# Norm chains between the stages: elementwise work moved from GpSimd to VectorE

## The chip, the cores and the metric

The kernel runs on one core of one Trainium2 chip, as one launch. The metric is the device time of that launch in microseconds (us). A core has a matrix engine (TensorE, PE in the profile; its weight loads are PEld), an engine for elementwise work on two inputs (VectorE, DVE), one for functions of one input with a scale and a bias (ScalarE, ACT), a programmable one that can do elementwise work too (GpSimd, POOL), and queues that start transfers (SyncE, SP, and POOL's own). Each engine runs its instructions strictly in the order in which they were written; engines wait for each other through semaphores. The order here is written by hand: no scheduler moves anything.

## What is computed

Two layers of a diffusion backbone over 640 tokens of width 1024: 128 context tokens and 512 latent tokens, which differ in their conditioning vector. Cut to what matters:

```
def layer(x, cond, l, P, ctx, rope):
    mods = (silu(cond) @ w_mod[l] + b_mod[l])            # 9 vectors: shift, 1+scale, gate, three times
    def pre(x_, s):
        return rmsnorm(x_, g_pre[l, s]) * (1 + mods[3*s+1]) + mods[3*s]
    f = swiglu(pre(x, 0), ...);  x = x + 0.5 * mods[2] * rmsnorm(f, g_post[l, 0])
    m = token_mix(pre(x, 1));    x = x +       mods[5] * rmsnorm(m, g_post[l, 1])
    f = swiglu(pre(x, 2), ...);  x = x + 0.5 * mods[8] * rmsnorm(f, g_post[l, 2])
```

So there are six stages (F, M, F, F, M, F: a feed-forward or the token mixer), and between two of them the same two norms: the sum of squares of the stage's output f gives r1, then x = x + gain * r1 * f; the sum of squares of the new x gives r2, and h = gain * r2 * x + shift is the next stage's input. All is fp32. A matrix product is made of three: each fp32 operand is split into a high part (rounded to the format that TensorE takes) and a low part (the rest), and high*high, high*low and low*high are added up.

## The kernel before

The activations lie transposed, features on the 128 partitions: a token array is 8 chunks (c = 0 to 7) of 128 x 640. The 640 tokens are worked in two halves of 320 columns. Half 0 holds the 128 context tokens and 192 latent ones, so an instruction with a gain for each kind of token falls into a 128-column and a 192-column one; half 1 is one piece of 320 columns.

Weights come by SP's queue into `raw`; `split` (line 240) makes the high part `wh` on ACT (a cast) and the low part `wl` on DVE (a subtraction, line 243). `run` goes through a list of tasks: each task first splits the weights that are wanted one or two tasks later, then writes deferred work (`flush`), then some steps of a generator that runs beside the matmuls (`step`), and at last its own matmuls. That order is the order on each engine.

At a boundary between two stages (`boundary`, line 533) the last products of the old stage (its tail) are made for a first half of the tokens, then for the second; the first half's norms run as the generator `chain` (line 401) beside the tail of the second half, and the second half's beside the head of the next stage. `STEPS` says how many steps of a chain stand before each task. A chain goes:

- `rms_r`: a product of ones with the squares (line 339) sums them over the partitions, then r1 on ACT and DVE (lines 321 to 329, `s` is r).
- Eight steps for x: POOL makes t = f * r1 (line 414, two chunks ahead), DVE x = t * gain + x (line 450; two instructions in half 0), and two chunks later ACT squares the new x (line 423) and the square is added to a sum (line 425): for the first half on DVE into one sum, for the second by turns on POOL and DVE into two sums.
- The product with ones again, now for r2.
- Eight steps for h. Odd chunks: DVE makes h = x * gain * r2 (line 488), ACT adds the shift and rounds to the high part (line 490), DVE makes the low part (line 505, one step later). Even chunks: POOL makes x * r2 (line 414), ACT (and DVE for the context tokens, line 496) applies gain and shift (line 498), ACT rounds (line 499), DVE subtracts (line 509).

`evac_branch` (line 516) takes a stage's output from PSUM: ACT copies it to f and squares it (line 528), POOL adds the squares up (line 529), for 7 of 8 chunks in each half. `sums` (line 627), at the beginning of each feed-forward, recombines the two parts of the input for a scheme that saves products: for each of 4 chunk pairs two adds of 128 x 640 on POOL (line 637), then four of 128 x 320 on DVE (lines 638 to 641) and a split. `x` and `f` are the slots A to D by turns, and the next input's high and low part (`hn`) are the two others.

After the last stage the boundary has only the x steps; there DVE does chunks 0 and 3 of the second half alone (`solo`: line 447 f * gain * r1, line 452 x + t), and POOL the other products.

Of the kernel before, what the change touches and what calls it, by code (L numbers as in the profile page):

```python
# [80 lines left out]
class Kernel:  # L81
# [319 lines left out]
    def chain(self, hf, ahead, kind, post=None, pre=None, out=None):  # L401


        nc = self.nc
        s = slice(hf * HW, (hf + 1) * HW)
        acc = self.acc[:, s]
        loc = lambda b, e: slice(b - hf * HW, e - hf * HW)
        nxt = None

        def scaled(src, c, r):  # L410
            if c >= KC:
                return None
            t = self.t3()
            nc.gpsimd.tensor_mul(t, src[:, c, s], r)
            return t


        accs = (acc,) if ahead else (self.ssq[:, s], acc)
        n = len(accs)

        def square(c, q):
            a = accs[c % n]
            nc.scalar.activation(a if c < n else q, self.x[:, c, s], AF.Square)
            if c >= n:
                (nc.vector if ahead or c % 2 else nc.gpsimd).tensor_add(a, a, q)

        if post is not None:
            l, st = post
            ge = self.co[l][:, 3 + st]
            r1 = self.R[:, s]  # L430
            self.rms_r(r1, (self.ssq[:, s],), 0.25 / D)

            solo = lambda c: pre is None and not ahead and c in (0, 3)
            q1 = lambda c: None if c < KC and solo(c) else scaled(self.f, c, r1)
            nxt = [q1(0), q1(1)]
            yield
        qs = []
        for c in range(KC):
            if post is not None:
                q = nxt.pop(0)  # L440
                nxt.append(q1(c + 2))
                if solo(c):
                    q = self.t3()
                for (b, e, cd) in self.segs(hf):
                    x, t, gain = self.x[:, c, b:e], q[:, loc(b, e)], ge[:, c, cd:cd + 1]
                    if solo(c):
                        nc.vector.scalar_tensor_tensor(t, self.f[:, c, b:e], gain, r1[:, loc(b, e)],
                                                       op0=ALU.mult, op1=ALU.mult)
                    else:
                        nc.vector.scalar_tensor_tensor(x, t, gain, x, op0=ALU.mult, op1=ALU.add)  # L450
                if solo(c):
                    nc.vector.tensor_add(self.x[:, c, s], self.x[:, c, s], q)
            if out is not None:
                nc.sync.dma_start(out[:, c, s], self.x[:, c, s])
            if pre is not None:
                qs.append((c, q))
                if len(qs) > LAG:
                    square(*qs.pop(0))
            yield
        if pre is None:  # L460
            return
        for q in qs:
            square(*q)
        yield
        l, st = pre
        r2 = self.R[:, s]
        self.rms_r(r2, accs, 1.0 / D)
        late = nxt = None

        alone = lambda c: c % 2 == 1  # L470

        def first(c):
            return scaled(self.x, c, r2) if c < KC and not alone(c) else None

        nxt = [first(0), first(1)]
        yield
        if self.hn is None:
            self.hn = (self.slot(self.hs[0], F32R), self.slot(self.hs[1], F32R))
        for c in range(KC + 1):
            new = None  # L480
            if c < KC:
                h = nxt.pop(0)
                nxt.append(first(c + 2))
                if alone(c):
                    h = self.t3()
                    for (b, e, cd) in self.segs(hf):
                        hs = h[:, loc(b, e)]
                        nc.vector.scalar_tensor_tensor(hs, self.x[:, c, b:e], self.co[l][:, st, c, cd:cd + 1],  # L488
                                                       r2[:, loc(b, e)], op0=ALU.mult, op1=ALU.mult)
                        nc.scalar.activation(self.hn[0][:, c, b:e], hs, AF.Identity, bias=self.shift(l, st, c, cd))  # L490
                else:
                    for (b, e, cd) in self.segs(hf):
                        hs = h[:, loc(b, e)]
                        gain, shift = self.co[l][:, st, c, cd:cd + 1], self.shift(l, st, c, cd)
                        if cd == 0:
                            nc.vector.tensor_scalar(hs, hs, gain, shift, op0=ALU.mult, op1=ALU.add)
                        else:
                            nc.scalar.activation(hs, hs, AF.Identity, bias=shift, scale=gain)
                    nc.scalar.copy(self.hn[0][:, c, s], h)
                new = (c, h)  # L500
            if late is not None:
                k, hk = late
                if alone(k):
                    for (b, e, cd) in self.segs(hf):
                        nc.vector.scalar_tensor_tensor(self.hn[1][:, k, b:e], hk[:, loc(b, e)], self.shift(l, st, k, cd),
                                                       self.hn[0][:, k, b:e].bitcast(F32),
                                                       op0=ALU.add, op1=ALU.subtract)
                else:
                    nc.vector.tensor_sub(self.hn[1][:, k, s], hk, self.hn[0][:, k, s].bitcast(F32))  # L509
            late = new  # L510
            yield
# [4 lines left out]
    def evac_branch(self, ps, c, hf):  # L516

        nc = self.nc
        s = slice(hf * HW, (hf + 1) * HW)
        nc.scalar.copy(self.f[:, c, s], ps[:, hf, :HW])  # L520
        f, ssq = self.f, self.ssq

        def squares():
            if c == 0:
                nc.scalar.activation(ssq[:, s], f[:, c, s], AF.Square)
            else:
                q = self.t3()
                nc.scalar.activation(q, f[:, c, s], AF.Square)
                nc.gpsimd.tensor_add(ssq[:, s], ssq[:, s], q)

        self.later.append(squares)

# [58 lines left out]
    def ffn(self, l, st, mod_todo, first=False):  # L591

        a, nc = self.a, self.nc
# [13 lines left out]
        def spill():  # L607

            nc.gpsimd.dma_start(self.d_x, self.x)
            self.gens["sums"] = sums()  # L610
# [16 lines left out]
        def sums():  # L627

            sa, sb = (self.slots.tile([P, 4, KC // 2, HW], F32R, tag=t, name=self.nm("s")) for t in (self.xs, self.fs))
            S["S"] = [(sa[:, i], sb[:, i]) for i in range(4)]  # L630
            one, two = slice(0, HW), slice(HW, T)
            f = lambda t: t.bitcast(F32)
            dve = nc.vector
            for k in range(KC // 2):
                a1, a2, s31, s24 = (self.t6() for _ in range(4))
                for d, c in ((a1, k), (a2, KC // 2 + k)):
                    nc.gpsimd.tensor_add(d, f(self.h[0][:, c, :]), f(self.h[1][:, c, :]))
                dve.tensor_sub(s31[:, two], a1[:, two], a2[:, two])
                dve.tensor_sub(s31[:, one], a1[:, one], a1[:, two])
                dve.tensor_sub(s24[:, one], s31[:, two], a1[:, one])  # L640
                dve.tensor_add(s24[:, two], a2[:, one], s24[:, one])
                yield
                v = lambda t: t.rearrange("p (a b) -> p a b", a=2)
                for i, t in ((2, s24), (0, s31)):
                    self.split(sa[:, i:i + 2, k, :], sb[:, i:i + 2, k, :], v(t))
                yield
# [120 lines left out]
        if first:  # L767
            def first_fn(*ws):
                p = [self.ps() for _ in ws]
                self.projs(list(zip(p, ws)), KC, self.h, (0, 1), hook=self.first_hook)  # L770
                self.advance(False, 5)
                self.st.close()
                begin()
                self.gens["sums"] = sums()
                new_act(0)
                gate_out(0, p[0], (0, 1))
                up_out(0, p[1], (0, 1))
                gate_out(1, p[2], (0, 1))
            mid.append(Task("first", first_fn, (wg[0, 0], wg[0, 1], wg[1, 0]), ahead=0))
            mid.append(up(1, 1, (0, 1)))  # L780
# [936 lines left out]
```

## Time and profile before

| | us |
|---|---|
| three runs: median (lowest to highest) | 3232.16 (3231.4 to 3234.57) |
| the profiled execution, its own time | 3228.82 |
| its span, first to last instruction | 3227.0 |
| TensorE busy | 3042.9 (94%) |
| VectorE busy | 2334.3 (72%) |
| ScalarE busy | 1436.4 (45%) |
| GpSimd busy | 1079.7 (33%) |
| mean granted TensorE clock | 0.981 of full |

How to read it: TensorE is busy nearly all the time, so what it waits is what can be won or lost, beside the 16 us after its last product; the waits lie in the boundaries, at the beginning and in a few other places. "PE ps L339 <- POOL s L425" means that TensorE's instruction of line 339 waited for GpSimd's of line 425. A row of a time line has the start, the duration and the engine, then line, operation, tiles (buffer numbers left out) and shapes; xN are N such instructions in a row, whose time is the sum. TensorE's clock has two levels, 2.4 GHz (1.00) and 1.2 GHz (0.50).

### The profile page before, as it was taken

To read this page: it belongs to the slowest core of one execution; us is meant where nothing else is said; L and a number is where in the kernel's file an instruction comes from. 1 tells how busy PE (TensorE), PEld (TensorE's weight loads), DVE (VectorE), ACT (ScalarE), POOL (GpSimd) and SP (SyncE) were. 2 spreads that over 40 slices of the span, in tenths; PEclk is the share of its full clock that TensorE was granted. 3 is DMA by queue.
4 is the path that set the end of the run, shared out by engine and by line. 5 is a ranking of instruction groups with operands and counts; after the bars stand their busy time and mean duration, and the time that the engine had idled before them with its cause. 6 is when DMAs were issued, how large, how long until landed. Compare 5 with 4: busy or idle time off the path is not lost. (4 is left out here: it accounts for less than half of the span.)

```text
span 3227.0 us, 51500 instructions
## 1 busy us (share of the span) xinstructions
PE 3042.9 (94%) x20278; PEld 2986.2 (93%) x20278; DVE 2334.3 (72%) x3282; ACT 1436.4 (45%) x2535; POOL 1079.7 (33%) x841
## 2 busy tenths in 40 slices
PE   7999998999999989999989999989999999899997
PEld 6999998899999979999979999979999998899997
DVE  7878768876666597787686788678666666866665
ACT  4344356454432354343554343564444324544344
POOL 4245344500011244354444354344000113343344
PEclk9999999999999999999999999999999999999999
DMA  4436653311234444536544436542111444345344
GB/s 178 166 110 186 165 169 119 133 58 60 68 112 148 154 150 158 158 118 175 181 152 157 151 119 179 180 152 93 60 55 61 144 140 163 139 133 140 104 130 153
DMA packets 140213, 433.45 MB, mean 134 GB/s; under 512 B 16834, under 2 KB 34050, under 8 KB 139076
## 3 DMA queue, kind: packets, MB, share of 16 engines
q1 hardware_dynamic: 119380, 351.34, 32.6%
q0 software_dynamic: 20304, 78.66, 9.1%
q8 instruction: 159, 2.61, 0.3%
q14 instruction: 82, 0.67, 0.1%
q10 hardware_dynamic: 288, 0.17, 0.0%
HBM read 377.51 MB, written 52.59 MB: 133 GB/s over the span
## 5 line engine op out<-in xcount | busy, mean ns | idle before, releaser
L243 DVE TENSOR_TENSOR wl<-raw,wh 128x1024 fp32r<-128x1024 f32 (+3 forms) x525 | 645.0, 1231 | 432.5 <-ACT wh L242 425.2
L311 PE MATMUL ps<-act,wh 128*128 128x320 f32 x2816 | 570.1, 313 | 29.5 <-DVE act L243 10.8
L242 ACT CAST wh<-raw 128x1024 fp32r<-128x1024 f32 (+3 forms) x525 | 481.2, 919 | 78.9 <-PE ps L311 39.1
L311 PEld LDWEIGHTS ps<-act,wh 128*128 128x128 f32 x2816 | 457.7, 190 | 38.2 <-DVE act L243 14.1
L665 PE MATMUL ps<-s,wh 128*128 128x320 f32 x1920 | 445.4, 311 | 26.7 <-DVE t L689 26.7
L375 DVE CUSTOM_DVE_ANT_0 t<-wm,sc,par 128x1024 bf16<-128x1024 f32 x256 | 373.2, 1493 | 10.0 <-DMA wm<-in_w_mod 9.9
L311 PE MATMUL ps<-slotA,wh 128*128 128x320 f32 x1312 | 366.4, 317 | 14.3 <-ACT wh L242 11.7
L311 PE MATMUL ps<-slotD,wh 128*128 128x320 f32 x1312 | 352.4, 316 | 20.7 <-DVE slotD L1528 15.0
L311 PE MATMUL ps<-slotA,wl 128*128 128x320 f32 x1312 | 363.5, 315 | 6.3 <-DVE wl L243 6.0
L311 PE MATMUL ps<-slotB,wh 128*128 128x320 f32 x1312 | 362.2, 314 | 3.0 <-DVE slotB L509 1.6
L311 PE MATMUL ps<-slotC,wh 128*128 128x320 f32 x1312 | 352.5, 317 | 7.1 <-ACT wh L242 3.2
L665 PEld LDWEIGHTS ps<-s,wh 128*128 128x128 f32 x1920 | 327.0, 188 | 32.8 <-ACT ps L672 22.2
L311 PE MATMUL ps<-act,wl 128*128 128x320 f32 x1408 | 355.0, 311 | 0.0
L665 PE MATMUL ps<-s,wl 128*128 128x320 f32 x960 | 298.0, 310 | 1.8 <-DVE wl L243 1.4
L311 PEld LDWEIGHTS ps<-slotD,wh 128*128 128x128 f32 x1312 | 236.9, 193 | 23.9 <-DVE slotD L1528 16.3
L311 PEld LDWEIGHTS ps<-slotA,wh 128*128 128x128 f32 x1312 | 239.1, 192 | 17.4 <-ACT wh L242 12.7
L311 PEld LDWEIGHTS ps<-slotA,wl 128*128 128x128 f32 x1312 | 239.1, 192 | 11.2 <-DVE wl L243 10.0
L311 PEld LDWEIGHTS ps<-act,wl 128*128 128x128 f32 x1408 | 246.9, 190 | 0.2
L311 PEld LDWEIGHTS ps<-slotC,wh 128*128 128x128 f32 x1312 | 236.9, 193 | 9.1 <-ACT wh L242 3.5
L311 PEld LDWEIGHTS ps<-slotB,wh 128*128 128x128 f32 x1312 | 239.0, 192 | 4.7 <-DVE slotB L509 2.1
L311 PE MATMUL ps<-slotC,wl 128*128 128x320 f32 x960 | 240.5, 316 | 1.4 <-DVE wl L243 1.0
L804 ACT COPY s<-ps 128x640 f32<-128x640 f32 x96 | 66.6, 694 | 297.0 <-issue 171.9
(341 smaller groups left out, 6461.9 us busy)
## 6 DMA issues: line engine op xcount, KB each, us to landing
raw<-in_w_gu SPq DMA_DIRECT2D x162, 512.0 KB, 3.8
wm<-in_w_mod SPq DMA_DIRECT2D x144, 512.0 KB, 4.7
raw<-in_w_dn SPq DMA_DIRECT2D x96, 384.0 KB, 3.2
raw<-in_w_gate SPq DMA_DIRECT2D x64, 512.0 KB, 3.6
d_f<-s POOLq DMA_DIRECT2D x96, 320.0 KB, 5.0
ru<-in_w_gu SPq DMA_DIRECT2D x60, 512.0 KB, 4.0
raw<-in_w_in SPq DMA_DIRECT2D x44, 512.0 KB, 3.4
raw<-in_w_dn SPq DMA_DIRECT2D x64, 320.0 KB, 2.9
```

The source lines that it names most:

```text
L242: self.nc.scalar.copy(h, src)
L243: self.nc.vector.tensor_sub(lo, src, h.bitcast(F32))
L311: nc.tensor.matmul(ps[:, hf, :HW], st[:, ws], m[:, k0 + k, hf * HW:(hf + 1) * HW], start=(first and k == 0 and i == 0), stop=(last and k = ...
L375: self.nc.vector.tensor_tensor_reduce(junk, wm, self.sc[:, j, :], 0.5, self.par[l][:, C_BMOD + ch:C_BMOD + ch + 1], ALU.mult, ALU.add, sel ...
L665: nc.tensor.matmul(o, w[x][:, ws], a[y][:, k, :], start=(new and k == 0 and i == 0), stop=(k == n - 1 and i == 2), skip_group_check=not new)
L804: nc.scalar.copy(t.rearrange("p (a b) -> p a b", a=2), ps[:, :, :HW])
```

## The change

In the boundaries that lead to another stage, DVE does all of the x steps as `solo` (f * gain * r1, then x + t; ACT and POOL have no product left) and all of the h steps as the odd chunks were. The squares of x go into one sum on DVE in both halves, those of the stage's output are added on DVE, and the first adds of `sums` are made on DVE. The last boundary keeps its products on GpSimd; its squares of f move.

```
-        accs = (acc,) if ahead else (self.ssq[:, s], acc)
+        accs = (acc,)
         n = len(accs)
         def square(c, q):
             a = accs[c % n]
             nc.scalar.activation(a if c < n else q, self.x[:, c, s], AF.Square)
             if c >= n:
-                (nc.vector if ahead or c % 2 else nc.gpsimd).tensor_add(a, a, q)
+                nc.vector.tensor_add(a, a, q)
...
-            solo = lambda c: pre is None and not ahead and c in (0, 3)
+            solo = lambda c: pre is not None or not ahead and c in (0, 3)
...
-        alone = lambda c: c % 2 == 1
+        alone = lambda c: True
...
                 q = self.t3()
                 nc.scalar.activation(q, f[:, c, s], AF.Square)
-                nc.gpsimd.tensor_add(ssq[:, s], ssq[:, s], q)
+                nc.vector.tensor_add(ssq[:, s], ssq[:, s], q)
...
                 for d, c in ((a1, k), (a2, KC // 2 + k)):
-                    nc.gpsimd.tensor_add(d, f(self.h[0][:, c, :]), f(self.h[1][:, c, :]))
+                    nc.vector.tensor_add(d, f(self.h[0][:, c, :]), f(self.h[1][:, c, :]))
```

Lines after the first edit stand two to four lower in the changed kernel: 446 is 447 before, 451 is 452, 424 is 425, 486 is 488, 503 is 505, 527 is 529, 635 is 637.

VectorE at the first mixer-to-feed-forward boundary, from r1 of the first half (half 0) on; slotC is f, slotD is x, s_1539 is r, s_1538 the sum of squares of x, s_1537 that of f, co the gains. Before:

```order
L450 SCALAR_TENSOR_TENSOR slotD_10705<-t_1589_11039,co_89,slotD_10705 128x128
L450 SCALAR_TENSOR_TENSOR slotD_10705<-t_1589_11039,co_89,slotD_10705 128x192
L243 TENSOR_TENSOR wl_11076<-raw_10985,wh_11075 128x1024
L450 SCALAR_TENSOR_TENSOR slotD_10705<-t_1590_11041,co_89,slotD_10705 128x128
L450 SCALAR_TENSOR_TENSOR slotD_10705<-t_1590_11041,co_89,slotD_10705 128x192
```

The same place in the changed kernel:

```order
L446 SCALAR_TENSOR_TENSOR t_1589_11039<-slotC_10704,co_89,s_1539_10709 128x128
L446 SCALAR_TENSOR_TENSOR t_1589_11039<-slotC_10704,co_89,s_1539_10709 128x192
L451 TENSOR_TENSOR slotD_10705<-slotD_10705,t_1589_11039 128x320
L243 TENSOR_TENSOR wl_11072<-raw_10985,wh_11071 128x1024
L527 TENSOR_TENSOR s_1537_10707<-s_1537_10707,t_1594_11075 128x320
L446 SCALAR_TENSOR_TENSOR t_1595_11078<-slotC_10704,co_89,s_1539_10709 128x128
L446 SCALAR_TENSOR_TENSOR t_1595_11078<-slotC_10704,co_89,s_1539_10709 128x192
L451 TENSOR_TENSOR slotD_10705<-slotD_10705,t_1595_11078 128x320
```

Each chunk has one more instruction of 320 columns and no longer takes a product t from GpSimd; the sum of the squares of f (line 527) stands behind the weight split and before the next chunk.

VectorE in the second half's steps for h at the first feed-forward-to-mixer boundary (half 0; slotA is x, slotC and slotD (before: 782, 783; after: 781, 782) the next input's parts), before:

```order
L496 TENSOR_SCALAR t_861_5408<-t_861_5408,co_89,mod_88 128x128
L488 SCALAR_TENSOR_TENSOR t_864_5444<-slotA_4212,co_89,s_670_4233 128x128
L488 SCALAR_TENSOR_TENSOR t_864_5444<-slotA_4212,co_89,s_670_4233 128x192
L509 TENSOR_TENSOR slotD_4932<-t_861_5408,slotC_4931 128x320
L496 TENSOR_SCALAR t_863_5439<-t_863_5439,co_89,mod_88 128x128
L505 SCALAR_TENSOR_TENSOR slotD_4932<-t_864_5444,mod_88,slotC_4931 128x128
L505 SCALAR_TENSOR_TENSOR slotD_4932<-t_864_5444,mod_88,slotC_4931 128x192
```

and in the changed kernel:

```order
L486 SCALAR_TENSOR_TENSOR t_862_5433<-slotA_4212,co_89,s_670_4233 128x128
L486 SCALAR_TENSOR_TENSOR t_862_5433<-slotA_4212,co_89,s_670_4233 128x192
L486 SCALAR_TENSOR_TENSOR t_863_5438<-slotA_4212,co_89,s_670_4233 128x128
L486 SCALAR_TENSOR_TENSOR t_863_5438<-slotA_4212,co_89,s_670_4233 128x192
L503 SCALAR_TENSOR_TENSOR slotD_4930<-t_862_5433,mod_88,slotC_4929 128x128
L503 SCALAR_TENSOR_TENSOR slotD_4930<-t_862_5433,mod_88,slotC_4929 128x192
```

An even chunk that took two instructions here (496 and 509) takes four.

## Rows read from the trace of the kernel before

**Rows 1.** The page's first part: busy time, share and instructions of each engine.
```profile
PE 3042.9 (94%) x20278; PEld 2986.2 (93%) x20278; DVE 2334.3 (72%) x3282; ACT 1436.4 (45%) x2535; POOL 1079.7 (33%) x841
```

**Rows 2.** Stretches around the five boundaries: length, busy by engine, clock, DMA, GB/s.
```profile
485.00:578.00 93.00, 77.91 (x461) 73.70 (x462) 77.32 (x118) 57.77 (x116) 42.77 (x45) 0.93 0.40 132
...
sum 469.00, PE 391.01 PEld 369.76 DVE 400.86 ACT 278.75 POOL 217.92; mean PE 78.20 PEld 73.95 DVE 80.17 ACT 55.75 POOL 43.58
```

**Rows 3.** TensorE's waits over the span: us in total, times, longest.
```profile
PE ps L311 <- ACT wh L242: 18.9, 6, 4.0
PE ps L339 <- DVE s L425: 16.0, 6, 5.5
...
PE ps L339 <- POOL s L425: 13.7, 5, 3.5
...
PE ps L311 <- ACT ps L815: 8.2, 6, 2.2
```

**Rows 4.** Time line of VectorE, first half's x steps, first mixer-to-feed-forward boundary.
```profile
1121.17 1.91 DVE L450 SCALAR_TENSOR_TENSOR slotD<-t,co,slotD 128x128 f32<-128x128 f32 x2 [1.00 <-POOL t L414]
1123.01 1.90 DVE L243 TENSOR_TENSOR wl<-raw,wh 128x1024 fp32r<-128x1024 f32 x1
...
1128.59 1.21 DVE L243 TENSOR_TENSOR wl<-raw,wh 128x1024 fp32r<-128x1024 f32 x1
1129.73 0.67 DVE L450 SCALAR_TENSOR_TENSOR slotD<-t,co,slotD 128x128 f32<-128x128 f32 x2
```

**Rows 5.** Time line of GpSimd in the same place.
```profile
1120.26 2.61 POOL L414 TENSOR_TENSOR t<-slotC,s 128x320 f32<-128x320 f32 x3 [5.75 <-DVE s L329]
```

**Rows 6.** Instructions of lines 425 and 637: min/median/max ns, first and last start.
```profile
L425 DVE TENSOR_TENSOR s<-s,t x50: 472/478/1162, 498.3 to 2772.2; 128x320 f32<-128x320 f32 x50
...
L425 POOL TENSOR_TENSOR s<-s,t x15: 925/1017/2517, 551.9 to 2771.8; 128x320 f32<-128x320 f32 x15
...
L637 POOL TENSOR_TENSOR t<-slotC,slotD x8: 1563/2011/2494, 86.3 to 135.0; 128x640 f32<-128x640 f32 x8
```

**Rows 7.** Three stretches of x steps, from r1 to the product for r2.
```profile
1120.20:1139.00 18.80, 13.02 (x87) 12.49 (x86) 17.58 (x26) 8.44 (x18) 11.18 (x11) 0.95 0.24 85
540.90:562.10 21.20, 17.56 (x119) 16.97 (x117) 20.20 (x27) 13.33 (x24) 15.85 (x18) 1.00 0.41 128
1162.90:1182.00 19.10, 15.45 (x104) 14.93 (x102) 18.80 (x24) 8.56 (x16) 13.52 (x11) 0.98 0.39 128
```

**Rows 8.** Time line of VectorE, first half's h steps, first feed-forward-to-mixer boundary.
```profile
519.82 1.17 DVE L505 SCALAR_TENSOR_TENSOR slotD<-t,mod,slotC 128x320 fp32r<-128x320 f32 x1
520.91 1.14 DVE L488 SCALAR_TENSOR_TENSOR t<-slotA,co,s 128x320 f32<-128x320 f32 x1
...
531.77 0.54 DVE L488 SCALAR_TENSOR_TENSOR t<-slotA,co,s 128x320 f32<-128x320 f32 x1
```

**Rows 9.** Time line of ScalarE in the same place.
```profile
518.07 0.83 ACT L242 CAST wh<-raw 128x768 fp32r<-128x768 f32 x1
...
522.08 0.56 ACT L490 ACTIVATE slotC<-t,mod 128x320 fp32r<-128x320 f32 x1 [1.77 <-DVE t L488]
...
523.22 1.04 ACT L242 CAST wh<-raw 128x1024 fp32r<-128x1024 f32 x1
```

**Rows 10.** Time line of VectorE after the first feed-forward's first products.
```profile
132.76 2.07 DVE L375 CUSTOM_DVE_ANT_0 t<-wm,sc,par 128x1024 bf16<-128x1024 f32 x1
...
134.76 1.27 DVE L375 CUSTOM_DVE_ANT_0 t<-wm,sc,par 128x1024 bf16<-128x1024 f32 x1
...
135.97 2.14 DVE L243 TENSOR_TENSOR wl<-raw,wh 128x640 fp32r<-128x640 f32 x1
138.03 0.81 DVE L243 TENSOR_TENSOR act<-t,act 128x640 fp32r<-128x640 f32 x1
```

**Rows 11.** Time line of TensorE in the same place.
```profile
138.90 0.63 PE L311 MATMUL ps<-act,wh 128*128 128x320 f32 x1 [4.39 <-DVE act L243]
```

**Rows 12.** The stretch after TensorE's wait of 5.5 us that ended at 1139.0.
```profile
1136.90:1143.80 6.90, 4.78 (x16) 4.39 (x17) 5.91 (x9) 5.20 (x11) 3.20 (x2) 0.51 0.43 142
```

## The prediction

> **What bounds the kernel now.** I read the busy times first: TensorE is busy 3042.9 us of the span of 3227.0 [rows 1], so 184.1 us are idle, and only idle time or a slow clock can be won or lost. Then the stretches around the five boundaries: in 469.0 us TensorE is busy 391.0, so 78.0 idle, 15.6 per boundary, while VectorE is busy 400.9 and GpSimd 217.9 [rows 2]. Third the waits [rows 3]: the product for r2 waits for VectorE's adds of line 425 (16.0) and for GpSimd's (13.7), and ordinary products wait for ScalarE's weight casts (18.9) and for its copies of line 815 (8.2). Last the time lines at those waits. The reader is to see there that VectorE is the engine that the boundary hangs on, and that it is slow while GpSimd works. At 1121.2 the two instructions of line 450 take 1.91 us, and the weight subtraction behind them 1.90, while GpSimd makes its products of 0.87 each (2.61/3) [rows 4, 5]; a few us later, with GpSimd's products done, the same pair takes 0.67 and the same subtraction 1.21. The instructions are the same; only their length differs.
>
> **The change part by part.** Each x step loses GpSimd's product and gains one VectorE add of 128x320 (0.478, from line 425's median [rows 6]; its product with gain and r1 has the form and length of line 450's). Each even h chunk loses GpSimd's product, one ScalarE pass and two short VectorE instructions and gets what an odd one has: two products and a subtraction. Line 527 (529 before) moves seven adds per half, line 424 four per second half, line 635 two adds of 128x640 per chunk pair, 32 in all. Added per boundary at undisturbed lengths: 8 + 8 adds x 0.48 = 7.7; eight even chunks, about 0.55 each more = 4.5; four squares 1.9; fourteen squares of f 6.7: 20.8 us, of which the seven squares of f that lie before the first half's r1 (3.4) run beside the tail of the first half, where no row shows TensorE waiting on VectorE. Against that stands the lengthening that goes. The sum by stages, each with its own cover:
>
> *First half's x steps, mixer to feed-forward (two boundaries).* The stretch is 18.8 us, VectorE busy 17.58 of it [rows 7], and the product behind it waits 5.5 [rows 3]. Afterwards: eight product pairs x 0.67 = 5.4, eight adds x 0.48 = 3.8, seven squares of x 3.4, three of f 1.4, three subtractions x 1.21 = 3.6: 17.6. In [rows 4] an instruction starts 0.07 before the one ahead ends (1128.59 + 1.21 against 1129.73); 29 times that is 2.0, so 15.6. At the end the last square on ScalarE and its add stand alone, about 1.1. That is 16.7: gain 2.1, twice 4.2.
>
> *First half, the other three boundaries.* The waits of the 16.0 that are not the two of 5.5 make 5.0 [rows 3]. GpSimd works there too and VectorE is lengthened likewise; I take 1.3 each, 3.9.
>
> *Second half's x steps.* Between feed-forward and the next stage the stretch is 21.2 [rows 7]. Afterwards eight pairs 5.4, eight adds 3.8, seven squares 3.4, seven subtractions at 1.21 8.5, a small one 0.5: 21.6, less 31 x 0.07 = 2.2, plus 1.1 at the end: 20.5, gain 0.7; thrice 2.1. GpSimd's add, up to 2.517 us [rows 6], is no longer what r2 waits for; VectorE's last square is. Behind a mixer the stretch is 19.1, VectorE busy 18.80 [rows 7]: eight products x 0.54, eight adds, seven squares, five subtractions and eight others (some 4.0) make 21.6, less 36 x 0.07, plus 1.1 less what overlaps the next cast: 19.6. A loss of 0.5, twice 1.0. Here the change has used up its cover.
>
> *First half's h steps.* VectorE has 1.17 + 1.14 to do here behind its weight subtraction, and the same product of 1.14 takes 0.54 later [rows 8]. The order makes a ring: ScalarE casts weights at 518.07 and next at 523.22, and between them its instruction of line 490 waits 1.77 for VectorE [rows 9]. Afterwards it has one add and three products, 0.48 + 3 x 0.54 = 2.10, less two more overlaps: 0.25 less per task, four tasks 1.0. The added wait is line 527's for ScalarE's square: it stands ahead of the next products and subtraction in VectorE's queue, but ScalarE's square follows the cast that the subtraction ahead of it needs, and is shorter than that subtraction, so it should be done by then. The even chunk's way at the start (GpSimd 0.87, two passes of ScalarE) becomes VectorE 0.54 and one pass of 0.56 [rows 5, 8, 9]: 0.33 + 0.56 = 0.9. Together 1.9 in three boundaries and, with two products per chunk, 1.4 in the other two: 8.5.
>
> *Second half's h steps.* No weight ring is as tight; the start's 0.9 and some of the lengthening, 1.2 in five: 6.0.
>
> *Sums.* At 138.9 TensorE waits 4.39 for VectorE's 138.03 instruction [rows 10, 11]. Ahead of it stand a dot of 2.07, whose twin took 1.27, and a subtraction of 2.14 that has the shape of the 0.81 one, both beside GpSimd's adds of 1.6 to 2.5 [rows 6]. The moved adds stand behind that instruction, so it comes 0.80 + 1.33 = 2.1 sooner. The other 28 adds (0.81 each) lie in feed-forward heads; there I charge 0.5 for each stage, -2.0, since VectorE is nearly full at the beginning of a head.
>
> *Clock.* After the 5.5 us wait TensorE runs 6.9 us at 0.51, the lower level [rows 12], busy 4.78, so about 2.4 us are lost. Where waits become shorter part of that comes back; 0.8 per boundary, 4.0.
>
> The last boundary keeps its GpSimd products; I take 0 there. Sum: 4.2 + 3.9 + 2.1 - 1.0 + 8.5 + 6.0 + 2.1 - 2.0 + 4.0 = 27.8. The profiled execution took 3228.8, so 3201.0; the median of the runs lies 3.3 higher, so 3204.
>
> *Bounds of what the trace does not show.* A VectorE add or product beside an idle GpSimd, with ScalarE and the transfers as they are: 0.48 at best, 1.16 at worst [rows 6]; I take the best, as the median of 50 is 0.478. An add of 128x640 on VectorE: 0.81 to 2.14 [rows 10], taken at 0.81. The clock term: 0 to 12 (five times 2.4).
>
> The rule to weigh here: the Trainium skill, "SBUF — State Buffer", section on the two sides, says that VectorE and GpSimd share a pair of ports as an exclusive lock, so that an instruction of one with two such operands blocks the other's for its whole length. The trace agrees with it: 1.91 against 0.67 [rows 4]. By that rule all of the lengthening goes with GpSimd's work and the sum stays; were the lengthening from something else, the slower rival below holds.
>
> **The rivals.** *VectorE becomes the bound.* If something other than GpSimd lengthens these instructions (the transfers that arrive, ScalarE), then VectorE gets 20.8 us more per boundary and keeps its length, in a stretch of 93.0 in which it is already busy 77.3 [rows 2]. It has 15.7 idle, so 5 us do not fit; in the ring of the h steps one add and three products of 1.15 (3.9) replace 2.31, 1.6 more for each of four tasks, 6.5. Taking 6.5 for each of five boundaries and 1 for the sums: 3228.8 + 33.5 + 3.3 = 3266. It decides from about 14 us of kept lengthening per boundary on. For it speaks that VectorE fills 85% of the boundaries; against it that the long forms end when GpSimd does [rows 4, 5, 8].
>
> *The waits hardly move.* The products of a boundary wait for ScalarE 27.1 us in casts and copies [rows 3], and the chain has more links on one engine: product, add, square, add, one after another. If the ring is paced by ScalarE and by the hand-overs, what VectorE saves becomes idle time: gain 0 to 4, about 3231. Against it: ScalarE itself waits 1.77 for VectorE in the ring [rows 9].
>
> *Nearly all of it goes.* If VectorE gets ahead of every task, the waits behind line 425 (29.7), some two thirds of the ScalarE waits that hang on VectorE (18) and 7 of the clock go: 55 less, 3177. Against it stand the summed stretches above, which are nearly as full after as before.
>
> **How the numbers follow.** Forecast 0.60, by itself 3190 to 3220 (the clock term from 0 to 12, the h steps from half to all, the sums from -4 to +4). Deep gain 0.14; no movement 0.14; slower 0.12. The range 3172 to 3238 holds the first three and leaves out most of the last. What a measurement of this kernel can tell from no change is about 0.2%, 6.5 us: 3225.7 to 3238.6. Faster than that: the forecast, the deep case and a quarter of the third, 0.78; within it 0.10; slower 0.12.
>
> **What would show it.** VectorE's pair at the mixer boundary's x steps at 0.67 throughout, subtractions of 1024 columns at 1.21 and line 424 at 0.48; GpSimd nearly empty in boundaries; the wait of 5.5 near 3.4; that of 4.39 near 2.3; the ring near 4.9 instead of 5.15; TensorE's idle time down by some 24. Wrong would be: pairs still near 1.9 (the first rival), or short instructions with gaps between them and waits as long as before (the second), or a new wait of ordinary products on VectorE in the heads of feed-forwards, where I charge only 0.5 each.

## The result, and the profile after

The changed kernel takes 3205.67 us (median of 6 runs, 3204.3 to 3208.43); the kernel before took 3231.76 in the same comparison (6 runs). The ratio is 0.9926, with a 95% interval of 0.9915 to 0.9937: some 24 us faster. The profiled execution took 3207.72 (span 3205.8), 21.1 less than that of before.

The page's first part of the changed kernel:

```profile
PE 3035.1 (95%) x20268; PEld 2980.0 (93%) x20268; DVE 2341.0 (73%) x3558; ACT 1423.2 (44%) x2515; POOL 756.8 (24%) x590
```

Against [rows 1]: VectorE has 276 instructions more and is busy 6.7 us longer, no more. GpSimd lost 251 instructions and 322.9 us. TensorE is idle 3205.8 - 3035.1 = 170.7 us, 13.4 less than before, and its busy time is 7.8 shorter (ten products with ones fewer, and less time at the lower clock).

TensorE's waits after (total, times, longest):

```profile
PE ps L339 <- DVE s L424: 35.8, 10, 4.3
...
PE ps L311 <- ACT wh L242: 9.6, 6, 2.9
...
PE ps L311 <- ACT ps L813: 7.3, 6, 1.7
PE ps L311 <- DVE act L243: 5.0, 9, 1.6
```

The casts' waits went from 18.9 to 9.6 [rows 3]; those for the sum of squares grew, from 16.0 + 13.7 = 29.7 to 35.8.

VectorE in the first half's x steps at the first mixer-to-feed-forward boundary, after:

```profile
1116.70 0.67 DVE L446 SCALAR_TENSOR_TENSOR t<-slotC,co,s 128x128 f32<-128x128 f32 x2
1117.41 0.49 DVE L451 TENSOR_TENSOR slotD<-slotD,t 128x320 f32<-128x320 f32 x1
1117.82 0.68 DVE L446 SCALAR_TENSOR_TENSOR t<-slotC,co,s 128x128 f32<-128x128 f32 x2
1118.53 0.49 DVE L451 TENSOR_TENSOR slotD<-slotD,t 128x320 f32<-128x320 f32 x1
1118.94 1.22 DVE L243 TENSOR_TENSOR wl<-raw,wh 128x1024 fp32r<-128x1024 f32 x1
```

Every length is the short one of [rows 4]. The starts show something new: the add begins at 1117.41, 0.04 after the end of the product that it reads (1116.70 + 0.67), where the instruction behind the add begins 0.08 before the add's end.

The three stretches of [rows 7] after, from r1 to the product for r2:

```profile
1114.00:1130.94 16.94, 12.64 (x87) 12.37 (x85) 16.37 (x38) 8.52 (x17) 0.00 (x0) 0.98 0.29 94
534.10:555.17 21.07, 17.24 (x118) 16.98 (x116) 19.51 (x40) 13.46 (x25) 1.98 (x11) 0.96 0.46 157
1155.90:1175.72 19.82, 15.43 (x104) 14.91 (x102) 19.23 (x36) 8.90 (x16) 0.54 (x1) 0.97 0.45 152
```

They were forecast as 16.7, 20.5 and 19.6.

ScalarE in the ring of the h steps, after:

```profile
512.09 0.83 ACT L242 CAST wh<-raw 128x768 fp32r<-128x768 f32 x1
...
514.81 0.56 ACT L488 ACTIVATE slotC<-t,mod 128x320 fp32r<-128x320 f32 x1 [1.52 <-DVE t L486]
515.73 0.56 ACT L488 ACTIVATE slotC<-t,mod 128x320 fp32r<-128x320 f32 x1 [0.36 <-DVE t L486]
...
516.87 1.04 ACT L242 CAST wh<-raw 128x1024 fp32r<-128x1024 f32 x1
```

From cast to cast it is 4.78, before 5.15 [rows 9]. ScalarE still waits for VectorE in it, 1.52 + 0.36 = 1.88 where it was 1.77; what went is ScalarE's own work, the one pass per even chunk.

VectorE and then TensorE at the first feed-forward's first products, after:

```profile
131.77 1.28 DVE L375 CUSTOM_DVE_ANT_0 t<-wm,sc,par 128x1024 bf16<-128x1024 f32 x1
...
134.18 0.82 DVE L243 TENSOR_TENSOR wl<-raw,wh 128x640 fp32r<-128x640 f32 x1
134.91 0.82 DVE L243 TENSOR_TENSOR act<-t,act 128x640 fp32r<-128x640 f32 x1
135.65 1.56 DVE L635 TENSOR_TENSOR t<-slotC,slotD 128x640 f32<-128x640 f32 x2
```

```profile
135.79 0.85 PE L311 MATMUL ps<-act,wh 128*128 128x320 f32 x4 [1.56 <-DVE act L243]
```

The dot and the subtraction lost 0.79 and 1.32 [rows 10], the wait went from 4.39 to 1.56 [rows 11].

Where the time was won is seen when TensorE's products other than those of line 339 (the ones with ones), 20204 in both traces, are paired one by one and the start in one trace is taken from that in the other (worked out from the two traces):

```
place (time in the kernel before)         us won there
first feed-forward, up to 250                   4.9
1st boundary, to the mixer, up to 620           1.2
2nd, to a feed-forward, up to 1250              3.4
3rd, between feed-forwards, up to 1760          4.2
4th, to the mixer, up to 2220                  -0.3
5th, to a feed-forward, up to 2850              7.5
last boundary                                  -0.6
```

The two boundaries that lead to a mixer, where no sums follow, gave almost nothing. These are two single traces: by the same pairing the kernel with only the sums moved, below, is 1.9 and 1.0 us sooner at these two places, where it differs in nothing, so a microsecond or two at one place says little.

### The profile page after: what moved, and what is told of

Same layout as the page of the kernel before. It is cut to its first block, busy times and chain, and to the rows that moved or that the text cites. A ratio compares the mean times of both kernels' runs of the same rounds, so it can differ in the third digit from the quotient of the medians.

```text
span 3205.8 us, 51353 instructions
## 1 busy us (share of the span) xinstructions
PE 3035.1 (95%) x20268; PEld 2980.0 (93%) x20268; DVE 2341.0 (73%) x3558; ACT 1423.2 (44%) x2515; POOL 756.8 (24%) x590
## 5 line engine op out<-in xcount | busy, mean ns | idle before, releaser
L243 DVE TENSOR_TENSOR wl<-raw,wh 128x1024 fp32r<-128x1024 f32 (+3 forms) x525 | 607.1, 1159 | 407.8 <-ACT wh L242 397.2
L375 DVE CUSTOM_DVE_ANT_0 t<-wm,sc,par 128x1024 bf16<-128x1024 f32 x256 | 369.9, 1480 | 11.6 <-DMA wm<-in_w_mod 11.4
L311 PEld LDWEIGHTS ps<-slotD,wh 128*128 128x128 f32 x1312 | 236.0, 192 | 20.5 <-DVE slotD L1526 16.3
```

Of the source, the lines that this page charges most:

```text
L243: self.nc.vector.tensor_sub(lo, src, h.bitcast(F32))
L311: nc.tensor.matmul(ps[:, hf, :HW], st[:, ws], m[:, k0 + k, hf * HW:(hf + 1) * HW], start=(first and k == 0 and i == 0), stop=(last and k = ...
L375: self.nc.vector.tensor_tensor_reduce(junk, wm, self.sc[:, j, :], 0.5, self.par[l][:, C_BMOD + ch:C_BMOD + ch + 1], ALU.mult, ALU.add, sel ...
```

## The experiments

Ratios are against the kernel before on the same chip, with 95% intervals; the changed kernel stands at 0.9926. A hundredth of a per cent is 0.32 us.

**One part alone.** The first four kernels are the kernel before with one part of the change each. The fifth part, the squares of x that go into one sum on VectorE, has no run of its own.

*x steps:*

```
-solo = lambda c: pre is None and not ahead and c in (0, 3)
+solo = lambda c: pre is not None or not ahead and c in (0, 3)
```

> The kernel before with only the x steps' products moved to VectorE. Theory A (GpSimd's elementwise instructions lengthen VectorE's, and each one taken away gives its share back by itself): about 8 us faster, 3224. Theory B (the lengthening has another source, so VectorE only gets 80 adds of 0.48 more): 5 to 15 us slower. Theory C (the parts pay only together, since the squares and h products left on GpSimd go on lengthening what stands beside them): within 3 us of the kernel before.

Measured: 1.0000 (0.9991 to 1.0009). No change, as theory C had it. A's 8 us did not come, nor did B's loss. The waits for the sum of squares did not shrink:

```profile
PE ps L339 <- DVE s L425: 22.0, 8, 4.8
...
PE ps L339 <- POOL s L425: 11.5, 5, 2.7
```

33.5 together, where the kernel before has 29.7.

*h steps:*

```
-alone = lambda c: c % 2 == 1
+alone = lambda c: True
```

> The kernel before with only the even chunks of the h steps moved to VectorE. Theory A: about 10 us faster, 3222, since GpSimd's first product no longer stands between r2 and the first chunk and the ring of the h steps gets shorter. Theory B: 5 to 15 us slower. Theory C: within 3 us of the kernel before.

Measured: 0.9989 (0.9980 to 0.9998), 3.6 us. In its trace the waits for casts are down:

```profile
PE ps L311 <- ACT wh L242: 11.4, 6, 3.1
```

7.5 less than before, and a smaller gain than that: in the same trace TensorE is busy 5.7 us longer with as many products (3048.6 against 3042.9), at a granted clock of 0.980 against 0.981.

*Squares of f:*

```
-nc.gpsimd.tensor_add(ssq[:, s], ssq[:, s], q)
+nc.vector.tensor_add(ssq[:, s], ssq[:, s], q)
```

> The kernel before with only the sums of the squares of f moved to VectorE. Theory A: within 4 us of the kernel before, since 6.7 us of VectorE per boundary stand against GpSimd's adds that lie mostly beside idle VectorE time. Theory B: 3 to 10 us slower. In either case it shows whether this part costs or pays by itself.

Measured: 0.9983 (0.9975 to 0.9992), 5.5 us faster. A little outside what A allowed, and the opposite of B.

*Sums:*

```
-nc.gpsimd.tensor_add(d, f(self.h[0][:, c, :]), f(self.h[1][:, c, :]))
+nc.vector.tensor_add(d, f(self.h[0][:, c, :]), f(self.h[1][:, c, :]))
```

> The kernel before with only the first adds of the sums moved to VectorE. Theory A: 5 us faster, nearly all of it at the first feed-forward, where the trace of the changed kernel is 4.9 us earlier after that place. Theory B (the 32 adds of 0.81 come on top): 2 to 8 us slower. If the four parts add up to about 26 us, they work apart; if to less than 20, the parts help each other.

Measured: 0.9963 (0.9950 to 0.9975), 12 us, more than twice the 5 expected: half of the whole gain from 32 instructions. Its trace ends 15.4 us sooner; 5.6 of that fell up to the end of the first feed-forward, 6.8 in the three boundaries that lead to the others, and 2.9 in the two that lead to a mixer, where this part changes nothing. The four parts add up to 0 + 3.6 + 5.5 + 12 = 21, near the whole 24, with an uncertainty of 3 to 4 us in each.

**One part undone.** Now the changed kernel with one part taken back (the diffs above, reversed).

> The changed kernel with the first adds of the sums back on GpSimd. Theory D (after the first four runs: half of the gain is the sums', whatever else moves): it loses 12 us against the changed kernel, so about 3218 where the kernel before has 3230. Theory A (the forecast's terms: the sums are worth 0, the chains 24): within 3 us of the changed kernel, about 3207.

Measured: 0.9984 (0.9975 to 0.9993), 18.7 us lost. Theory D named the right part, too small; A's terms are refuted. GpSimd, VectorE and TensorE of this kernel at the head behind the first mixer:

```profile
1191.70 1.81 POOL L635 TENSOR_TENSOR t<-slotA,slotB 128x640 f32<-128x640 f32 x1 [12.22 <-DVE slotB L503]
1202.69 1.75 POOL L635 TENSOR_TENSOR t<-slotA,slotB 128x640 f32<-128x640 f32 x1 [9.18 <-DVE act L243]
```

```profile
1191.99 1.87 DVE L503 SCALAR_TENSOR_TENSOR slotB<-t,mod,slotA 128x320 fp32r<-128x320 f32 x1
...
1203.00 2.51 DVE L243 TENSOR_TENSOR wl<-raw,wh 128x1024 fp32r<-128x1024 f32 x1
```

```profile
1196.23 0.42 PE L311 MATMUL ps<-slotA,wh 128*128 128x320 f32 x1 [1.53 <-ACT wh L242]
...
1205.57 0.41 PE L311 MATMUL ps<-slotA,wl 128*128 128x320 f32 x1 [1.22 <-DVE wl L243]
```

Two adds of GpSimd start here, and the VectorE instruction beside each takes 1.3 us longer: the low part of a chunk of h, 0.54 elsewhere, takes 1.87, and a subtraction of 1.22 takes 2.51. At the same two products the changed kernel's TensorE waits 0.21 and not at all; here it waits 1.53 and 1.22. The second wait is for the long subtraction itself. The first is for a cast on ScalarE that stands behind an instruction which waits 1.68 for VectorE (0.36 in the changed kernel). Outside this part of the work nothing moved: the ten chains from r1 to the product for r2 take 189.6 us in sum in this trace and 189.7 in the changed kernel's.

> The changed kernel with the even chunks of the h steps back on GpSimd. Theory D (each part by itself): it loses 3.5 us, about 3210 where the kernel before has 3230. Theory A (the h steps carry 14.5 us of the forecast): it loses 12 to 15 us, about 3220.

Measured: 0.9909 (0.9894 to 0.9925). Not the loss of 12 to 15 that A had, and not D's 3.5 either; it is rather faster than the changed kernel, though the intervals overlap.

> The changed kernel with the products of the x steps back on GpSimd, the sums of squares staying on VectorE. Theory D (the x steps alone moved nothing): within 3 us of the changed kernel, about 3206 where the kernel before has 3230. Theory C (the x steps pay only with the rest, when no other GpSimd work is left beside them): it loses 6 to 10 us, about 3215.

Measured: 0.9939 (0.9927 to 0.9951), 4 us behind the changed kernel with overlapping intervals. That lies between D and C and decides neither.

**The lengthening by itself.** Here GpSimd's load is brought back without the work being moved. In the changed kernel:

```
+idle = lambda c: nc.gpsimd.tensor_mul(self.ssq[:, s], self.f[:, c, s], r1) if pre is not None else None
...
                 if solo(c):
                     q = self.t3()
+                idle(c)
```

> The changed kernel, and beside each of its x steps (80 in all) GpSimd makes the product f * r1 again as the kernel before did, into the half of the old sum of squares that is dead by then; nobody reads it. VectorE's work is the changed kernel's. Theory A (GpSimd's work is what lengthens VectorE's): VectorE's instructions beside it go to some 1.1 us again, each chain gets 4 to 6 us longer, and the kernel loses 20 to 40 us against the changed one: 3227 to 3245 where the kernel before has 3229. Theory B (the lengthening has another source, GpSimd's is a coincidence): no change, 3206.

Measured: 1.0054 (1.0042 to 1.0067), 3246.83 us: 41 us slower than the changed kernel, at the far end of A. Its page, first part, and VectorE and GpSimd beside each other:

```profile
PE 3046.3 (94%) x20268; PEld 2988.3 (92%) x20268; DVE 2385.6 (74%) x3558; ACT 1422.7 (44%) x2515; POOL 845.0 (26%) x670
```

```profile
1120.51 1.31 DVE L448 SCALAR_TENSOR_TENSOR t<-slotC,co,s 128x128 f32<-128x128 f32 x2
1121.85 1.05 DVE L453 TENSOR_TENSOR slotD<-slotD,t 128x320 f32<-128x320 f32 x1
1122.83 1.90 DVE L243 TENSOR_TENSOR wl<-raw,wh 128x1024 fp32r<-128x1024 f32 x1
1124.65 1.16 DVE L529 TENSOR_TENSOR s<-s,t 128x320 f32<-128x320 f32 x1
```

```profile
1120.65 8.90 POOL L434 TENSOR_TENSOR s<-slotC,s 128x320 f32<-128x320 f32 x8 [40.42 <-DVE s L329]
```

The same 3558 VectorE instructions are busy 44.6 us longer, 0.56 for each of the 80 idle products; the ten chains from r1 to the product for r2 are longer by the same amount (189.7 to 234.3 in sum, worked out from the two traces), and the kernel's time follows almost one to one. That GpSimd's products are the source, and what one costs on average, is shown.

In the next kernel `tensor_mul` became `memset(self.ssq[:, s], 0.0)`.

> As idle_products, but GpSimd fills the same 128x320 with zeros instead of multiplying, so it is busy at the same places and writes as much, and reads nothing. If reading is what holds VectorE up (as the Trainium skill has it, SBUF — State Buffer, on the two sides of the memory: two-input VectorE instructions block only against a GpSimd instruction that reads): no change against the changed kernel, 3206, and lengths of 0.48 and 0.54 beside the fills. If any GpSimd instruction with such a tile holds it up: VectorE lengthened as in idle_products, 10 to 40 us lost.

Measured: 0.9926 (0.9913 to 0.9938), the changed kernel's own ratio. GpSimd and VectorE:

```profile
1107.92 3.32 POOL L434 MEMSET s<- 128x320 f32 x8 [35.38 <-PE ps L339]
```

```profile
1108.77 1.23 DVE L243 TENSOR_TENSOR wl<-raw,wh 128x1024 fp32r<-128x1024 f32 x1 [1.90 <-ACT wh L242]
1110.15 0.50 DVE L325 SCALAR_TENSOR_TENSOR t<-t,t 128x320 f32<-128x320 f32 x1 [0.16 <-ACT t L322]
1110.75 0.49 DVE L326 SCALAR_TENSOR_TENSOR s<-t,s 128x320 f32<-128x320 f32 x1
```

The subtraction and the two short instructions lie wholly or partly beside fills and have their undisturbed lengths. So it is in the whole trace: 59 two-input VectorE instructions lie beside fills for more than 0.1 us, and none differs by more than 0.01 us from the same instruction of the changed kernel (worked out from the two traces). The Trainium skill ("SBUF — State Buffer", the section on the two sides) restricts the block on two-input VectorE instructions to GpSimd instructions that read, and this agrees. The test is weaker than the one before it: from start to start a fill takes 0.42 and a product 1.11, and the fills waited for nothing of r1 and so ran ahead of the x steps here.

**Versions that beat both.** The 0.12 between a product and its add suggested writing the next chunk's product first:

```
-                for (b, e, cd) in self.segs(hf):            # product of chunk c
-                    ...
-                nc.vector.tensor_add(self.x[:, c, s], self.x[:, c, s], q)
+                nxt.append(mine(c + 1))                     # product of chunk c + 1
+                nc.vector.tensor_add(self.x[:, c, s], self.x[:, c, s], q)
```

> The changed kernel, with the product of the next chunk written ahead of the add of this one in the x steps, so that no VectorE instruction reads what the one just ahead of it wrote. In the changed kernel's trace an add behind its own product starts 0.04 us after that product's end, other instructions 0.08 before it: 0.12 per chunk, 1.0 per chain of eight. If VectorE's length of the chain sets the wait for the sum of squares (35.8 us in the changed kernel), 5 to 10 us faster than the changed kernel, about 3199 where the kernel before has 3230. If the chain is paced by something else (ScalarE's squares, the tail's tasks), no change, about 3206.

Measured: 0.9880 (0.9867 to 0.9894), 3189.12 us, 15 us faster than the changed kernel and more than expected. VectorE:

```profile
1111.34 0.67 DVE L440 SCALAR_TENSOR_TENSOR t<-slotC,co,s 128x128 f32<-128x128 f32 x2
1111.93 0.48 DVE L454 TENSOR_TENSOR slotD<-slotD,t 128x320 f32<-128x320 f32 x1
1112.33 0.67 DVE L440 SCALAR_TENSOR_TENSOR t<-slotC,co,s 128x128 f32<-128x128 f32 x2
1112.92 0.48 DVE L454 TENSOR_TENSOR slotD<-slotD,t 128x320 f32<-128x320 f32 x1
```

```profile
PE ps L339 <- DVE s L424: 26.1, 10, 3.3
```

A chunk takes 0.99 (1112.33 to 1111.34) instead of 1.12 (1117.82 to 1116.70), and the wait for the sum of squares fell by 9.7. The ten chains are 9.8 us shorter in sum (189.7 to 179.9, worked out from the two traces), where 80 pairs at 0.12 make 9.6, so the pairs account for the whole shortening. TensorE's busy time fell too, by 6.6 (3035.1 to 3028.5).

> The staggered kernel with the even chunks of the h steps back on GpSimd. If the lower time of undo_h against the changed kernel (0.9909 against 0.9926) was real: about 5 us faster than staggered, 0.986 of the kernel before, 3185. If it was scatter: 0.988, 3190, or slower, as the h steps on GpSimd lengthen VectorE in the ring.

Measured: 0.9869 (0.9854 to 0.9884). Between the two expectations, 3.6 us from staggered and with overlapping intervals: whether the even h chunks do better on GpSimd stays open for the whole kernel. That they are worth 14 us on VectorE is refuted twice.

```
+            if c >= KC - 2:
+                accs.append(q)          # the square of chunk 6 or 7 goes to the product with ones
-            if c >= n:
+            elif c >= n:
                 nc.vector.tensor_add(a, a, q)
```

> The staggered kernel with the squares of the last two chunks not added on VectorE but given to TensorE's product with ones as two more terms. If VectorE's last adds set the wait for the sum of squares of x: 4 to 9 us faster than staggered, 0.986, 3184, since TensorE waits at that place anyway. If TensorE's four more products per chain (0.35 each) are not hidden: 0 to 7 us slower than staggered, 3190 to 3197.

Measured: 0.9846 (0.9832 to 0.9859), 3180.05 us, 11 us faster than staggered. The wait is down to

```profile
PE ps L339 <- DVE s L426: 9.9, 7, 2.3
```

This is the fastest version: 1.54% under the kernel before, twice what the change gave.

## Why the number was right and its terms were not

The forecast was 27.8 us less on the profiled execution; by the ratio it is 0.0074 x 3228.8 = 23.9. The time and the cause, GpSimd's instructions lengthening VectorE's, were right, and the slower rival's condition (a lengthening from elsewhere) is refuted by idle_products. The shares were wrong, and their errors cancelled: that the sum came out close is luck. Of the signs that the forecast named, TensorE's idle time fell by 13.4 and not by some 24, and the wait of 5.5 fell to 4.3 and not to 3.4; and the wait for the sum of squares behaved as the rival "The waits hardly move" had it.

The stretches of the five boundaries, added up (us, worked out from the traces), show which part moved what. A chain goes from r1 to the product for r2; "between" is from the first half's product for r2 to the second half's r1, with the first half's h steps in it; "rest" is all other time, with the second half's h steps and the sums, and its scatter between single traces is some 4 us (2873.3 in the changed kernel, 2876.9 with the idle fills, whose chains and "between" are the same within 0.6).

```
kernel            first chains  between  second chains    rest
before                    94.3    141.1          100.5  2891.2
changed                   87.0    142.9          102.7  2873.3
x steps alone             88.9    143.1           96.0  2895.8
h steps alone             93.4    143.1          100.5  2888.4
squares of f alone        92.7    136.1          100.9  2894.2
sums alone                93.1    140.4          100.4  2877.7
sums taken back           87.0    143.1          102.7  2888.3
h steps taken back        87.0    137.9          102.7  2867.7
x steps taken back        91.8    137.6          104.0  2869.4
```

*x steps (forecast 9.2; alone 0, taken back 4).* The three stretches of [rows 7] were forecast well (0.2 to 0.6 us off), and the first chains got 7.3 shorter where the sum has 8.1. The second chains, forecast 1.1 shorter, got 2.2 longer: the x steps alone shorten them by 4.4, and the rest of the change, most likely the squares of x, takes that back (not shown, as that part has no run of its own); and "thrice 2.1" took the stretch behind the third boundary for one of 21.2, where it was 19.8 and became 20.9. What failed beyond that is the step from a shorter chain to a shorter kernel. With the x steps alone the ten chains lose 9.8 us, and the time does not move; what takes it back outside the chains is not shown. The wait is no measure of it either. In the kernel before, TensorE at the first boundary had these two waits ahead of its product for r2:

```profile
499.70 0.41 PE L311 MATMUL ps<-act,wh 128*128 128x320 f32 x1 [1.09 <-ACT act L242]
500.97 0.57 PE L311 MATMUL ps<-act,wh 128*128 128x320 f32 x2 [0.71 <-DVE act L243]
```

In the changed kernel they are 0.17 and 0.22. TensorE reaches the product sooner, by these 1.4 us and by the time at the lower clock that used to follow (granted clock 0.80 from 501.0 to 509.4), while the chain got only 1.5 us shorter (19.2 to 17.7, from r1 to the product's start); the wait there went from 1.26 to 2.99 and the lower clock now follows it (0.60 from 502.6 to 506.2). What was won in the tail was waited for at its end. And for VectorE as a whole the price per chunk was even: an idle product costs it 0.56, an add costs it 0.49 - 0.08 + 0.12 = 0.53, and with the x steps alone it has 80 instructions more and is busy 3.4 us less.

*h steps (forecast 14.5; alone 3.6, taken back none or negative).* The ring did get shorter, by more than was forecast (4.78 against 4.9; by the forecast's own terms, 2.31 against 2.10 less 0.14, it was 0.35 per task and not 0.25). What failed is the step from the ring to the stretch that holds it: "between" went from 141.1 to 143.1 with the h steps alone, and with them taken back it is 137.9 against 142.9 (135.5 against 140.5 in stag_h and staggered). On GpSimd this stretch is the shorter one; what sets its length is not shown. The forecast also let nothing else take from the same waits, but the sums' adds prolong them: for the casts 18.9 before, 11.4 with the h steps alone, 11.7 with the sums alone, 9.6 with everything. I added terms that share one wait.

*Sums (forecast 0.1; alone 12, taken back 18.7).* This is the term that was mis-sized most. I saw at the first feed-forward that GpSimd's add held VectorE up by 2.1, yet "in feed-forward heads; there I charge 0.5 for each stage": I priced what the moved adds cost VectorE there and not what they had cost on GpSimd. That is 1.3 us for each of the two instructions shown above, against 0.80 that the add costs on VectorE itself (two of them, from 135.65 on, end with the next start, at 137.24). These two are long ones: with the sums taken back the 32 adds lengthen VectorE's instructions by 29.2 us, 0.91 each, and VectorE is busy only 3.6 us longer (2344.6 against 2341.0), while the kernel loses 18.7 (15.2 between the two traces, nearly all of it in "rest"). So the price per add is nearly even here too, and most of the difference lies in which instruction pays: on VectorE the add stands behind the urgent one, as at 135.65, and on GpSimd it starts when its input is there and lengthens whatever stands beside it. The rows show this at three places; for the others it is argued.

*Squares of f (forecast 0; alone 5.5).* Moved alone they make VectorE busy 16.2 us longer (2350.5) and yet "between" 5.0 shorter. The forecast priced only what they cost VectorE; how they gain is not shown.

*Clock (forecast 4.0).* TensorE's busy time fell by 7.8, part of it the ten products fewer; the lower clock followed the wait of 4.31 as it had followed that of 5.5 [rows 12], so at this place little of it came back; how much of the 7.8 is the clock's was not separated:

```profile
1130.94:1136.90 5.96, 5.96 (x20) 5.56 (x21) 5.59 (x9) 3.55 (x8) 0.00 (x0) 0.50 0.50 159
```

The deep rival (3177) needed VectorE ahead of every task. It was not, but stag_pe shows that the waits it spoke of could be had, by shortening the chain itself.

## What to carry to other kernels

Price an instruction on GpSimd by what it adds to the VectorE instruction beside it, and by whether that one is waited for; here 32 large adds at the heads of the feed-forwards were worth more than 80 smaller products in the chains, though on either engine both cost VectorE about the same. A wait is not a price, for it can grow while the end comes sooner; chains shorter by 9.8 us gave nothing in one kernel and came with 15 us in another, and terms that rest on one wait are not to be added. A forecast that comes out right is not yet an explanation: take the parts back one by one.

## What was not expected of the hardware

- A VectorE instruction that reads what the one ahead of it wrote starts 0.04 us after that one's end, others 0.08 before it. The 0.12 is small, but 80 such pairs were 9.6 us of chain, and the kernel written without them is 15 us faster.
- A GpSimd product lengthened VectorE by 0.56 us on average, though it takes 1.11 itself, an add of 128x640 by 0.91, and GpSimd's fills by nothing that the trace shows.
